# Two MLPs with a Strassen-scheme down-projection on one Trainium2 core: VectorE and ScalarE held to the order of the source, with one sum, gathering or addition behind the split of each plain tile

## The chip, the core and the metric

The kernel runs on one core of one Trainium2 chip. The metric is device time in microseconds (us) of one execution; the time before is the median of three runs, 2092.59 us (2090.18 to 2093.03). Engines are named as the profile names them: PE is TensorE's matmul, PEld its weight load, DVE is VectorE, ACT is ScalarE, POOL is GpSimd, SP is SyncE, which here only issues DMAs.

## What is computed

Two layers of a transformer trunk over 256 tokens of width 2048, in fp32. Layer 0 mixes tokens by stick-breaking attention, layer 1 by an indexer that selects keys for a softmax attention. Behind each mixer stands the MLP, which is what the change touches:

```python
SEQ, D_MODEL = 256, 2048
D_FF = 4 * D_MODEL
for i in range(DEPTH):                       # DEPTH = 2
    ...
    h = rms_norm(x, norm_mlp[i])
    x = x + jnp.square(jax.nn.relu(h @ w_up[i])) @ w_down[i]
```

## The kernel before

**Tiles and the split.** All weights stream through the core as tiles of 256 rows by 512 columns (512 KB), each used once. A tile lands in one of five `wraw` buffers (`load`, line 966; issued on SP's queue in program order). `split` (line 978) turns it into two fp32r halves: ACT copies it to `wh` (line 988, recorded as line 87, the helper `copy`), and DVE writes `wl`, the rest, as `raw - wh` (line 989). `wh` and `wl` have three buffers each, and a tile is split two tiles ahead of its use (`LEAD = 2`). PE takes eight matmuls with `wh` and then four with `wl` for a plain tile (`high_first`, line 246), over both halves of the tokens.

**The loop** (line 1008) runs over a flat list of `Item`s, one for each tile. For item i it emits the split of item i+2, the load of item i+7, the matmuls of item i, the functions in `it.post`, and what was put off by `later` (work that turns an activation: `to_features` transposes on DVE, writes the result to DRAM in four DMAs `td<-jx`, reads it back as `jx<-td` four items on, and runs a DVE and an ACT step behind that).

**Order.** The program is built under a scheduler that models the time of each engine and may set an instruction ahead of others on its queue. `keep` (line 80) holds an instruction in the program's order among the others that were kept; `pin` (line 82) does so only for the first 24 items. So in the MLPs before, the splits (`pin`) are placed by the scheduler, and so are the DVE operations of the Strassen scheme.

**The MLP** (`mlp`, line 327) works through d_ff in four quarters f. `up(f)` makes the quarter's activation `hT`, `down(f)` multiplies it by `w_down`, two column blocks of 512 at a time: `down_pair(f, n)` (line 405). Of the quarter's eight row blocks, blocks 0 and 2 (`SEVEN`) are done for both column blocks and both token halves by Strassen's seven products in place of eight. A pair is 19 tiles: twelve plain ones, `G0` to `G5` and `H0` to `H5` (twelve matmuls each, line 419), and the seven products `s1` to `s7` (six matmuls each, line 437). `s1`, `s2`, `s3` use tiles as they are, `s5`, `s6`, `s7`, `s4` use sums of tiles:

- `t1` (line 464): X = Y - raw(s1), where Y is a fourth tile, loaded by itself (`load_y`);
- `t2` (line 467): Z = raw(s3) - X; `t3` (line 468): Y = raw(s3) - Y; `t4` (line 471): Z = raw(s2) - Z;
- s5 takes X, s6 and later s4 take Z, s7 takes Y. They are split like any tile, but have no load.

The products of s1, s6, s5, s7 are gathered from PSUM into E: `p1` (an ACT copy, line 475), `p6` (line 478), `p5` (line 481), `p7` (line 485). `into(t)` (line 491) adds E to the residual `xs`, and `down_done` (line 361) adds the plain accumulators, by `add_residual` (line 309). `sums(f)` (line 387) builds the sums of activations once a quarter. The order of a pair's tiles is the list `TURNS` (line 49):

```python
TURNS = "G0 H0 s1 G1 s3 H1 G2 s6 s5 H2 s7 G3 H3 s2 G4 H4 s4 G5 H5".split()
```

There are 15 pairs: two in each of four quarters in layer 0, and seven in layer 1, whose last two column blocks are done plainly. In layer 0's last quarter `add_residual` also turns the finished columns for the next mixer (`turn`, line 188). In the first pair of quarters 0 to 2 there is still work of the up-projection left: two times the squared ReLU (line 347), the ACT copy (line 352) and the DVE rest (line 357), and a pair of transposes (line 167).

Of the kernel before, what the change touches and what calls it, by code (L numbers as in the profile page):

```python
# [9 lines left out]
F32 = mybir.dt.float32  # L10
# [7 lines left out]
P = 128  # L18
# [27 lines left out]
WARM = 8  # L46
SEVEN = (0, 2)
STEP = KB * (SEVEN[1] - SEVEN[0])
TURNS = "G0 H0 s1 G1 s3 H1 G2 s6 s5 H2 s7 G3 H3 s2 G4 H4 s4 G5 H5".split()


class Item:
# [2 lines left out]

    def __init__(self, src, a, b, mm):
        self.src, self.a, self.b, self.mm, self.post = src, a, b, mm, []
        self.form, self.after, self.early = None, None, []


@with_exitstack
def trunk(ctx, tc, x, x_t, gains_t, w_in_a, w_out_a, w_in_b, w_out_b, rel_bias, w_up, w_down, out):
# [23 lines left out]
    def copy(o, i, scale=1.0):  # L86
        pin(act.activation(o, i, AF.Copy, scale=scale))  # L87
# [168 lines left out]
    def tokens_out(items, key, w, r0, c0, lhs, q, done, apart=False, alone=False):  # L256
# [25 lines left out]
        def mm(wh, wl):  # L282
# [10 lines left out]
            for t, j, part, wx, a, z in high_first(wh, wl):  # L293
# [2 lines left out]
                    start=a and q == 0, stop=z and q == (end if t else QB) - 1))  # L296
        it = Item(rows(w, r0 + KB * P * q, KB * P, c0, 512), KB, 512,
                  mm if len(items) >= LEAD else first)
        if q == QB - 1:
            it.post.append(lambda: done(accs.pop(key)))  # L300
        items.append(it)
# [25 lines left out]
    def mlp(l, next_col):  # L327
# [77 lines left out]
        def down_pair(f, n):  # L405
# [22 lines left out]
            def seventh(left, src, to=None, done=None):  # L428


                def mm(wh, wl):
                    if to is None:
                        p = auxp.tile([P, 512], F32, name="aux")
                    else:
                        p = accs[keys[to[0]]][to[1]]
                    for t, j, part, wx, a, z in high_first(wh, wl, 1):
                        keep(pe.matmul(p, left(part, j), wx[:, j, :], start=to is None and a,  # L437
                                       stop=to is None and z))
                    if done is not None:
                        done(p)  # L440
# [19 lines left out]
            def load_y():  # L460
                keep(nc.sync.dma_start(new("Y"), block(1, qa)))

            def t1(b11):
                dve.tensor_sub(new("X"), sec["Y"], b11)  # L464

            def t2_t3(b22):
                dve.tensor_sub(new("Z"), b22, sec["X"])
                dve.tensor_sub(sec["Y"], b22, sec["Y"])

            def t4(b21):  # L470
                dve.tensor_sub(sec["Z"], b21, sec["Z"])  # L471

            def p1(p):
                sec["E"] = sec["pool"].tile([P, 4, 512], F32, name="E", bufs=1)
                copy(sec["E"][:, 0], p)

            def p6(p):
                dve.tensor_add(sec["E"][:, 1], p, sec["E"][:, 0])

            def p5(p):  # L480
                dve.tensor_add(sec["E"][:, 2], p, sec["E"][:, 1])

            def p7(p):
                E = sec["E"].rearrange("p (a b) e -> p a b e", a=2)
                dve.tensor_add(E[:, :, 1], p.unsqueeze(1).to_broadcast([P, 2, 512]),
                               sec["E"][:, 1:3])

            def into(t):
                xc = xs[:, t, 1024 * n:1024 * n + 1024].rearrange("p (c e) -> p c e", c=2)
                E = sec["E"].rearrange("p (c t) e -> p c t e", t=2)[:, :, t]  # L490
                dve.scalar_tensor_tensor(xc, E, sec["rs2"][:, t:t + 1], xc, op0=OP.mult, op1=OP.add)

            qa, qb = SEVEN
            seven = {
                "s1": seventh(own(qa, 0), block(0, qa), None, p1),
                "s2": seventh(own(qb, 0), block(0, qb), (0, 0)),
                "s3": seventh(summed(3), block(1, qb), (1, 0)),
                "s4": seventh(own(qb, 1), "Z", (0, 1)),
                "s5": seventh(summed(0), "X", None, p5),
                "s6": seventh(summed(1), "Z", None, p6),  # L500
                "s7": seventh(summed(2), "Y", None, p7)}
# [476 lines left out]
    def split(i, a=slice(None)):  # L978
        if i < len(items):
            it = items[i]  # L980
            raw = raws[i] if it.form is None else it.form()
            if it.form is None and a.stop in (None, it.a):
                raws.pop(i)
            if i not in parts:
                parts[i] = [wpool.tile([P, WT], F32R, name=name)[:, :it.a * it.b].rearrange(
                    "p (a b) -> p a b", a=it.a) for name in ("wh", "wl")]
            wh, wl = parts[i]
            copy(wh[:, a], raw[:, a])
            pin(dve.tensor_sub(wl[:, a], raw[:, a], wh[:, a].bitcast(F32)))  # L989
# [66 lines left out]
```

## Time and profile before

| | |
|---|---|
| median of three runs | 2092.59 us |
| time of the profiled execution | 2085.87 us |
| its span, first to last instruction | 2084.2 us |
| mean granted TensorE clock | 0.999 |
| ACT busy, share of the span | 49% |
| POOL busy, share of the span | 1% |
| DMA, mean | 223 GB/s |

The profile is of one execution. A busy time on PE is a sum over instructions that overlap: a matmul is recorded with some 390 ns, and the next one starts 227 ns behind it. "Idle before" is the time an engine stood still ahead of an instruction, and the name behind the arrow is what ended that. In the timeline, neighbouring instructions of a kind are merged into one row with their count.

### The profile page before, as it was taken

The page shows a single profiled execution, that of the slowest core. Times are in us where ns is not written, and L with a number is a line of the kernel's source. Part 1 is how long each engine was busy: PE and PEld are TensorE (multiplying, and loading weights), DVE is VectorE, ACT ScalarE, POOL GpSimd, SP SyncE. Part 2 cuts the span into 40 slices and gives each one's busy share as a digit, 9 for nine tenths or more (in the row PEclk, how much of TensorE's full clock was granted, in tenths as well). Part 3 has the DMA queues.
Part 4 walks back from the last instruction along what each step waited for, and adds up shares of the span by engine and source line. Part 5 has one row for each costly group of instructions (what it writes and reads, how often), then busy time and mean ns, then how long its engine had stood idle before and what let it go on. Part 6 is the DMA issues. An engine that isn't in the chain of part 4 may idle for free. (4 is left out here: it accounts for less than half of the span.)

```text
span 2084.2 us, 24925 instructions
## 1 busy us (share of the span) xinstructions
PE 2062.2 (99%) x9164; PEld 1696.2 (81%) x9164; DVE 1449.8 (70%) x1581; ACT 1025.5 (49%) x1233; POOL 29.0 (1%) x71
## 2 busy tenths in 40 slices
PE   9999999999999999999999999999999999999999
PEld 7888888888878878878877788888887887888787
DVE  5555655666686687688785798676668667867875
ACT  6555554544454444455454566554445444444543
POOL 0010100000000000000000000000000000000000
PEclk9999999999999999999999999999999999999999
DMA  9878847887856866776588688497876687577554
GB/s 314 241 224 223 240 154 227 242 253 231 248 197 198 261 200 199 235 220 204 192 231 250 198 246 260 151 269 231 253 238 216 198 236 229 191 218 246 194 198 164
DMA packets 477467, 464.85 MB, mean 223 GB/s; under 512 B 269664, under 2 KB 279968, under 8 KB 477344
## 3 DMA queue, kind: packets, MB, share of 16 engines
q1 hardware_dynamic: 469488, 455.81, 71.5%
q10 hardware_dynamic: 7856, 7.45, 1.3%
q8 instruction: 72, 1.18, 0.2%
q14 instruction: 51, 0.42, 0.1%
HBM read 425.90 MB, written 37.22 MB: 222 GB/s over the span
## 5 line engine op out<-in xcount | busy, mean ns | idle before, releaser
L87 ACT ACTIVATE wh<-wraw 128x1024 fp32r<-128x1024 f32 (+1 forms) x725 | 765.6, 1057 | 887.0 <-PE acc L294 571.8
L989 DVE TENSOR_TENSOR wl<-wraw,wh 128x1024 fp32r<-128x1024 f32 (+1 forms) x725 | 877.1, 1218 | 433.9 <-ACT wh L87 417.4
L294 PE MATMUL acc<-wh,xT 128*128 128x512 f32 x3264 | 811.7, 390 | 2.3 <-ACT xT L198 2.3
L294 PEld LDWEIGHTS acc<-wh,xT 128*128 128x128 f32 x3264 | 610.8, 188 | 130.5 <-ACT xT L198 2.5
L294 PE MATMUL acc<-wl,xT 128*128 128x512 f32 x1632 | 437.4, 390 | 0.0
L294 PEld LDWEIGHTS acc<-wl,xT 128*128 128x128 f32 x1632 | 306.2, 188 | 64.1 <-DVE wl L989 0.3
L419 PE MATMUL acc<-wh,hT 128*128 128x512 f32 x1440 | 357.1, 390 | 0.0
L419 PEld LDWEIGHTS acc<-wh,hT 128*128 128x128 f32 x1440 | 271.2, 188 | 57.4
L419 PE MATMUL acc<-wl,hT 128*128 128x512 f32 x720 | 194.0, 391 | 2.0 <-DVE wl L989 1.9
L419 PEld LDWEIGHTS acc<-wl,hT 128*128 128x128 f32 x720 | 134.1, 188 | 34.0 <-DVE wl L989 6.6
L294 PE MATMUL acc<-wh,oT 128*128 128x512 f32 x512 | 128.9, 391 | 0.0
L294 PEld LDWEIGHTS acc<-wh,oT 128*128 128x128 f32 x512 | 95.5, 188 | 19.8
L294 PE MATMUL acc<-wl,oT 128*128 128x512 f32 x256 | 69.5, 392 | 0.0
L167 DVE STREAM_TRANSPOSE jx<-acc 128x512 f32<-128x512 f32 x68 | 44.6, 695 | 34.5 <-PE acc L294 31.9
L294 PEld LDWEIGHTS acc<-wl,oT 128*128 128x128 f32 x256 | 47.8, 188 | 9.8
L471 DVE TENSOR_TENSOR Z<-wraw,Z 128x1024 f32<-128x1024 f32 x15 | 18.4, 1226 | 44.9 <-DMA wraw<-in_w_down_dram 44.9
L437 PE MATMUL aux<-wh,S 128*128 128x512 f32 x180 | 48.2, 389 | 0.0
L87 ACT ACTIVATE wh<-Z 128x1024 fp32r<-128x1024 f32 x30 | 31.9, 1063 | 27.9 <-PE acc L437 17.2
L352 ACT ACTIVATE hT<-jx 128x1024 fp32r<-128x1024 f32 x32 | 33.8, 1055 | 23.4 <-DVE jx L347 23.4
L464 DVE TENSOR_TENSOR X<-Y,wraw 128x1024 f32<-128x1024 f32 x15 | 18.4, 1226 | 36.9 <-DMA wraw<-in_w_down_dram 36.9
L309 DVE SCALAR_TENSOR_TENSOR xs<-acc,rs,xs 128x512 f32<-128x512 f32 x56 | 39.3, 743 | 5.0 <-PE acc L419 5.0
L989 DVE TENSOR_TENSOR wl<-Z,wh 128x1024 fp32r<-128x1024 f32 x30 | 36.7, 1223 | 7.5 <-ACT wh L87 7.4
(191 smaller groups left out, 1275.1 us busy)
## 6 DMA issues: line engine op xcount, KB each, us to landing
wraw<-in_w_up_dram SPq DMA_DIRECT2D x256, 512.0 KB, 4.3
wraw<-in_w_down_dram SPq DMA_DIRECT2D x241, 512.0 KB, 4.8
wraw<-in_w_in_a_dram SPq DMA_DIRECT2D x94, 512.0 KB, 4.5
wraw<-in_w_in_b_dram SPq DMA_DIRECT2D x64, 512.0 KB, 4.4
td<-jx SPq DMA_DIRECT2D x240, 128.0 KB, 4.3
jx<-td SPq DMA_DIRECT2D x45, 512.0 KB, 6.2
wraw<-in_w_out_a_dram SPq DMA_DIRECT2D x32, 512.0 KB, 4.3
wraw<-in_w_out_b_dram SPq DMA_DIRECT2D x32, 512.0 KB, 4.6
```

The source lines that it names most:

```text
L87: pin(act.activation(o, i, AF.Copy, scale=scale))
L167: dve.transpose(y[:, m:m + k, :].rearrange("p k f -> p (k f)"), part)
L294: (keep if alone else pin)(pe.matmul(acc[t], L[:, KB * q + j, part, t * P:(t + 1) * P], wx[:, j, :], start=a and q == 0, stop=z and q == ( ...
L309: dve.scalar_tensor_tensor(xc, acc[t], scale[:, t:t + 1], xc, op0=OP.mult, op1=OP.add)
L352: keep(act.activation(h, r, AF.Copy))
L419: keep(pe.matmul(acc[t], L[:, KB * qs[i] + j, part, t * P:(t + 1) * P], wx[:, j, :], start=a and i == 0, stop=z and i == len(qs) - 1))
L437: keep(pe.matmul(p, left(part, j), wx[:, j, :], start=to is None and a, stop=to is None and z))
L464: dve.tensor_sub(new("X"), sec["Y"], b11)
L471: dve.tensor_sub(sec["Z"], b21, sec["Z"])
L989: pin(dve.tensor_sub(wl[:, a], raw[:, a], wh[:, a].bitcast(F32)))
```

## The change

Four things are changed. `TURNS` sets `H2` between s6 and s5, and s5 and s7 each behind another plain tile. The splits of all MLP tiles are kept in program order on ACT and DVE (`it.alone`, set for the tiles of `up`, of the plain column blocks and of the pairs), and so are `t1` to `t4`, `p1`, `p6`, `p5`, `p7` and `into`. These no longer hang on the split or the product that they belong to (`it.after`, `done`), but on named tiles of the pair, one behind each, through `it.post.insert(0, step)`. And `t2` and `t3`, which were one function, are two.

```diff
-TURNS = "G0 H0 s1 G1 s3 H1 G2 s6 s5 H2 s7 G3 H3 s2 G4 H4 s4 G5 H5".split()
+TURNS = "G0 H0 s1 G1 s3 H1 G2 s6 H2 s5 G3 s7 H3 s2 G4 H4 s4 G5 H5".split()
...
-            def t1(b11):
-                dve.tensor_sub(new("X"), sec["Y"], b11)
-
-            def t2_t3(b22):
-                dve.tensor_sub(new("Z"), b22, sec["X"])
-                dve.tensor_sub(sec["Y"], b22, sec["Y"])
...
+            def t1():
+                keep(dve.tensor_sub(new("X"), sec["Y"], seven["s1"].raw))
+
+            def t2():
+                keep(dve.tensor_sub(new("Z"), seven["s3"].raw, sec["X"]))
+
+            def t3():
+                keep(dve.tensor_sub(sec["Y"], seven["s3"].raw, sec["Y"]))
...
-            seven["s1"].after, seven["s3"].after, seven["s2"].after = t1, t2_t3, t4
             for name in TURNS:
                 it = seven[name] if name in seven else plain("GH".index(name[0]), int(name[1]))
+                it.alone = True
                 items.append(it)
             items[base - 8].early.append(load_y)
-            for t in range(2):
-                items[base + TURNS.index(("G3", "H3")[t])].post.append(lambda t=t: into(t))
+            for name, step in (("H0", t1), ("s1", p1), ("G1", t2), ("H1", t3), ("H2", p6), ("G3", p5),
+                               ("H3", t4), ("G4", p7), ("H4", lambda: into(0)),
+                               ("G5", lambda: into(1))):
+                items[base + TURNS.index(name)].post.insert(0, step)
...
-            copy(wh[:, a], raw[:, a])
-            pin(dve.tensor_sub(wl[:, a], raw[:, a], wh[:, a].bitcast(F32)))
-            if it.after is not None:
-                it.after(raw)
+            order = keep if it.alone else pin
+            order(act.activation(wh[:, a], raw[:, a], AF.Copy))
+            order(dve.tensor_sub(wl[:, a], raw[:, a], wh[:, a].bitcast(F32)))
+            it.raw = raw
```

The two programs have the same number of instructions of each kind on each engine. How DVE's queue is ordered by them is shown at three places. In the rows below a tile's buffer carries a running number; a split is the row that writes `wl`, and its `wraw` says which tile it is. Line numbers of the changed kernel are larger by up to seven.

The first place is DVE's queue at the start of the first pair of layer 0's second quarter. Before: `wraw_5509` is G0, 5528 H0, 5547 s1, 5565 G1, 5585 s3.

```order
L464 TENSOR_TENSOR X_5643<-Y_5485,wraw_5547 128x1024
L989 TENSOR_TENSOR wl_5600<-wraw_5509,wh_5599 128x1024
L347 SCALAR_TENSOR_TENSOR jx_5579<-jx_5579 128x1024
L467 TENSOR_TENSOR Z_5685<-wraw_5585,X_5643 128x1024
L468 TENSOR_TENSOR Y_5485<-wraw_5585,Y_5485 128x1024
L989 TENSOR_TENSOR wl_5618<-wraw_5528,wh_5617 128x1024
L167 STREAM_TRANSPOSE jx_5635<-acc_5487 128x512 x2
L989 TENSOR_TENSOR wl_5640<-wraw_5547,wh_5639 128x1024
L989 TENSOR_TENSOR wl_5664<-wraw_5565,wh_5663 128x1024
L357 TENSOR_TENSOR hT_5339<-jx_5579,hT_5339 128x2x4x128
L989 TENSOR_TENSOR wl_5682<-wraw_5585,wh_5681 128x1024
```

Now, at the same place, 5547 again being s1, 5565 G1, 5585 s3, 5603 H1, 5621 G2, and the split of `Z` the one for s6:

```order
L996 TENSOR_TENSOR wl_5640<-wraw_5547,wh_5639 128x1024
L348 SCALAR_TENSOR_TENSOR jx_5579<-jx_5579 128x1024
L996 TENSOR_TENSOR wl_5662<-wraw_5565,wh_5661 128x1024
L464 TENSOR_TENSOR X_5680<-Y_5485,wraw_5547 128x1024
L996 TENSOR_TENSOR wl_5684<-wraw_5585,wh_5683 128x1024
L358 TENSOR_TENSOR hT_5339<-jx_5579,hT_5339 128x2x4x128
L996 TENSOR_TENSOR wl_5698<-wraw_5603,wh_5697 128x1024
L467 TENSOR_TENSOR Z_5715<-wraw_5585,X_5680 128x1024
L996 TENSOR_TENSOR wl_5718<-wraw_5621,wh_5717 128x1024
L996 TENSOR_TENSOR wl_5730<-Z_5715,wh_5729 128x1024
L470 TENSOR_TENSOR Y_5485<-wraw_5585,Y_5485 128x1024
```

`t1`, which reads s1's tile, stood ahead of the splits of G0, H0 and s1 itself, and now stands behind those of s1 and G1; `t2` and `t3`, which read s3's tile, stood ahead of the split of H0, and now stand behind those of H1 and s6.

The second place is DVE's queue in the middle of the same pair. Before, `wraw_5752` is s2, 5688 H2, 5720 G3, `jx` is an activation on its way to the squared ReLU:

```order
L989 TENSOR_TENSOR wl_5717<-wraw_5621,wh_5716 128x1024
L989 TENSOR_TENSOR wl_5731<-Z_5685,wh_5730 128x1024
L989 TENSOR_TENSOR wl_5749<-X_5643,wh_5748 128x1024
L471 TENSOR_TENSOR Z_5685<-wraw_5752,Z_5685 128x1024
L989 TENSOR_TENSOR wl_5767<-wraw_5688,wh_5766 128x1024
L478 TENSOR_TENSOR E_5697<-aux_5772,E_5697 128x512
L989 TENSOR_TENSOR wl_5781<-Y_5485,wh_5780 128x1024
L481 TENSOR_TENSOR E_5697<-aux_5786,E_5697 128x512
L347 SCALAR_TENSOR_TENSOR jx_5728<-jx_5728 128x1024
L989 TENSOR_TENSOR wl_5796<-wraw_5720,wh_5795 128x1024
```

Now, with 5701 G3, 5733 H3, 5752 s2, 5770 G4, 5783 H4:

```order
L996 TENSOR_TENSOR wl_5780<-wraw_5701,wh_5779 128x1024
L480 TENSOR_TENSOR E_5694<-aux_5772,E_5694 128x512
L348 SCALAR_TENSOR_TENSOR jx_5727<-jx_5727 128x1024
L996 TENSOR_TENSOR wl_5800<-Y_5485,wh_5799 128x1024
L996 TENSOR_TENSOR wl_5812<-wraw_5733,wh_5811 128x1024
L483 TENSOR_TENSOR E_5694<-aux_5803,E_5694 128x512
L358 TENSOR_TENSOR hT_5339<-jx_5727,hT_5339 128x2x4x128
L996 TENSOR_TENSOR wl_5832<-wraw_5752,wh_5831 128x1024
L996 TENSOR_TENSOR wl_5847<-wraw_5770,wh_5846 128x1024
L473 TENSOR_TENSOR Z_5715<-wraw_5752,Z_5715 128x1024
L996 TENSOR_TENSOR wl_5866<-wraw_5783,wh_5865 128x1024
L996 TENSOR_TENSOR wl_5878<-Z_5715,wh_5877 128x1024
```

`t4`, which reads s2's tile, stood ahead of the splits of H2, s7, G3, H3 and s2 itself, and now stands behind those of s2 and G4. Between `p6` and `p5`, where one split stood, there are two.

The third place is DVE's queue where layer 0's MLP ends and the second mixer begins (`acc_7915` and `acc_7936` are the last two column blocks, `xs` the residual, the transposes of `xs` feed the turn for the mixer; `wraw_8152` and `wraw_8164` are the mixer's second and third tile). Before:

```order
L309 SCALAR_TENSOR_TENSOR xs_89<-acc_7915,rs2_3294,xs_89 128x512 x2
L989 TENSOR_TENSOR wl_8237<-wraw_8152,wh_8236 128x1024
L167 STREAM_TRANSPOSE jx_8228<-xs_89 128x512 x2
L309 SCALAR_TENSOR_TENSOR xs_89<-acc_7936,rs2_3294,xs_89 128x512 x2
L691 TENSOR_TENSOR gqk_8281<-gains_74 128x1
L989 TENSOR_TENSOR wl_8284<-wraw_8164,wh_8283 128x1024
L167 STREAM_TRANSPOSE jx_8256<-xs_89 128x512 x2
```

Now, the first column block being `acc_7913`:

```order
L310 SCALAR_TENSOR_TENSOR xs_89<-acc_7913,rs2_3294,xs_89 128x512
L996 TENSOR_TENSOR wl_8237<-wraw_8149,wh_8236 128x1024
L310 SCALAR_TENSOR_TENSOR xs_89<-acc_7913,rs2_3294,xs_89 128x512
L167 STREAM_TRANSPOSE jx_8228<-xs_89 128x512
L310 SCALAR_TENSOR_TENSOR xs_89<-acc_7936,rs2_3294,xs_89 128x512 x2
L697 TENSOR_TENSOR gqk_8281<-gains_74 128x1
L996 TENSOR_TENSOR wl_8284<-wraw_8161,wh_8283 128x1024
L167 STREAM_TRANSPOSE jx_8228<-xs_89 128x512
L167 STREAM_TRANSPOSE jx_8256<-xs_89 128x512 x2
```

The addition of the first block and its transposes, which stood together but for one split, are taken apart: half of the addition, a split, the other half, one transpose, the second block's addition, another split, the other transpose. On SP's queue the load that stood between the two writes of the turned columns now stands ahead of both, and in layer 0's last pair the write of the second block turned there has moved ahead of two loads. In the other pairs SP's order is as it was.

More of the change, by code (lines that the diff above doesn't have):

```diff
@@ L57, in __init__ @@
         self.src, self.a, self.b, self.mm, self.post = src, a, b, mm, []
-        self.form, self.after, self.early = None, None, []
+        self.form, self.early, self.alone, self.raw = None, [], False, None
 @with_exitstack
@@ L298, in tokens_out @@
                   mm if len(items) >= LEAD else first)
+        it.alone = alone
         if q == QB - 1:
@@ L426, in plain, with seventh @@
                 return it
-            def seventh(left, src, to=None, done=None):
+            def seventh(left, src, to=None):
                 def mm(wh, wl):
@@ L438, in mm @@
                                        stop=to is None and z))
-                    if done is not None:
-                        done(p)
+                    it.product = p
                 own_rows = not isinstance(src, str)
@@ L461, in load_y, with t4, p1, p6 @@
                 keep(nc.sync.dma_start(new("Y"), block(1, qa)))
-            def t1(b11):
-                dve.tensor_sub(new("X"), sec["Y"], b11)
-            def t2_t3(b22):
-                dve.tensor_sub(new("Z"), b22, sec["X"])
-                dve.tensor_sub(sec["Y"], b22, sec["Y"])
-            def t4(b21):
-                dve.tensor_sub(sec["Z"], b21, sec["Z"])
-            def p1(p):
-                sec["E"] = sec["pool"].tile([P, 4, 512], F32, name="E", bufs=1)
[L475 to L483, printed above, removed]
+            def t1():
[4 more added lines that the diff above has]
+                keep(dve.tensor_sub(sec["Y"], seven["s3"].raw, sec["Y"]))
+            def t4():
+                keep(dve.tensor_sub(sec["Z"], seven["s2"].raw, sec["Z"]))
+            def p1():
+                sec["E"] = sec["pool"].tile([P, 4, 512], F32, name="E", bufs=1)
+                keep(act.activation(sec["E"][:, 0], seven["s1"].product, AF.Copy))
+            def p6():
+                keep(dve.tensor_add(sec["E"][:, 1], seven["s6"].product, sec["E"][:, 0]))
+            def p5():
+                keep(dve.tensor_add(sec["E"][:, 2], seven["s5"].product, sec["E"][:, 1]))
+            def p7():
                 E = sec["E"].rearrange("p (a b) e -> p a b e", a=2)
-                dve.tensor_add(E[:, :, 1], p.unsqueeze(1).to_broadcast([P, 2, 512]),
-                               sec["E"][:, 1:3])
+                keep(dve.tensor_add(E[:, :, 1],
+                                    seven["s7"].product.unsqueeze(1).to_broadcast([P, 2, 512]),
+                                    sec["E"][:, 1:3]))
             def into(t):
@@ L490, in into @@
                 E = sec["E"].rearrange("p (c t) e -> p c t e", t=2)[:, :, t]
-                dve.scalar_tensor_tensor(xc, E, sec["rs2"][:, t:t + 1], xc, op0=OP.mult, op1=OP.add)
+                keep(dve.scalar_tensor_tensor(xc, E, sec["rs2"][:, t:t + 1], xc,
+                                              op0=OP.mult, op1=OP.add))
             qa, qb = SEVEN
             seven = {
-                "s1": seventh(own(qa, 0), block(0, qa), None, p1),
+                "s1": seventh(own(qa, 0), block(0, qa)),
                 "s2": seventh(own(qb, 0), block(0, qb), (0, 0)),
```

6 lines of the change are left out of this document (3 added, 3 removed).

## The prediction, made before the changed kernel had run

> **What bounds the kernel now.** The page's part 1 comes first, then the list of waits of DVE, then PE over the stretches in which the down-projections run.
>
> ```profile
> PE 2062.2 (99%) x9164; PEld 1696.2 (81%) x9164; DVE 1449.8 (70%) x1581; ACT 1025.5 (49%) x1233; POOL 29.0 (1%) x71
> ...
> core 0: us, PE busy (x), PEclk, DMA share, GB/s
> 556.95:643.00 86.05, 84.94 (x374) 1.00 0.63 202
> ...
> sum 656.44, PE 641.53; mean PE 106.92
> ...
> 702.84 1.98 PE L294 MATMUL acc<-wh,xT 128*128 128x512 f32 x8
> ...
> 721.88 1.98 PE L294 MATMUL acc<-wh,xT 128*128 128x512 f32 x8
> ...
> 735.48 1.07 PE L437 MATMUL aux<-wh,hT 128*128 128x512 f32 x4
> 736.38 0.61 PE L437 MATMUL aux<-wl,hT 128*128 128x512 f32 x2
> 736.84 1.98 PE L419 MATMUL acc<-wh,hT 128*128 128x512 f32 x8
> ```
>
> PE is the bound. In the up-projection seven plain tiles lie between 702.84 and 721.88: 2.720 us each, 0.2267 us for a matmul; a product of Strassen's scheme, with six, takes 1.36 (735.48 to 736.84). The six stretches in which L419 and L437 run alone (15 pairs of 12 x 12 + 7 x 6 = 186 matmuls, 2790 in all) have 656.44 us. At 0.2267 they would need 632.4. So **24.0 us are lost in the pairs**, and nothing that keeps PE's work can gain more there.
>
> ```profile
> DVE Z L471 <- DMA wraw<-in_w_down_dram: 44.9, 15, 3.8
> DVE X L464 <- DMA wraw<-in_w_down_dram: 36.9, 15, 4.1
> ...
> DVE Z L467 <- DMA wraw<-in_w_down_dram: 4.6, 5, 1.6
> ...
> 749.08 1.23 DVE L471 TENSOR_TENSOR Z<-wraw,Z 128x1024 f32<-128x1024 f32 x1 [3.83 <-DMA wraw<-in_w_down_dram]
> 750.23 1.22 DVE L989 TENSOR_TENSOR wl<-wraw,wh 128x1024 fp32r<-128x1024 f32 x1
> 751.36 0.68 DVE L478 TENSOR_TENSOR E<-aux,E 128x512 f32<-128x512 f32 x1
> ...
> 751.50 1.20 PE L419 MATMUL acc<-wl,hT 128*128 128x512 f32 x4 [0.45 <-DVE wl L989]
> ```
>
> Who loses them is read here. DVE stood 86.4 us before `t4`, `t1` and `t2`, once or more in each of the 15 pairs, waiting for tiles that PE needs much later. At 749.08 it had waited 3.83 us for s2's tile, with H2's split queued behind; that split ended at 751.45, and PE's four `wl` matmuls of H2 began at 751.50.
>
> **What the change takes away.** `t1` to `t4` now stand behind the split of the tile that they read, so that tile has landed when they come up, and the 86.4 us of waits go. What is late next is DVE's own work, so I walk through one pair. A `wl` may start when ACT's `wh` is done, and that starts when PE has left the buffer:
>
> ```profile
> 702.13 1.06 ACT L87 ACTIVATE wh<-wraw 128x1024 fp32r<-128x1024 f32 x1 [1.66 <-PE acc L294]
> ...
> 703.22 1.23 DVE L989 TENSOR_TENSOR wl<-wraw,wh 128x1024 fp32r<-128x1024 f32 x1 [1.49 <-ACT wh L87]
> ...
> 736.58 1.07 ACT L87 ACTIVATE wh<-wraw 128x1024 fp32r<-128x1024 f32 x1 [0.75 <-PE aux L437]
> ```
>
> Against the start of PE's tile i, ACT starts the split of tile i+2 0.71 us ahead behind a plain tile (702.13 to 702.84) and 0.26 ahead behind a product (736.58 to 736.84). PE needs a plain tile's `wl` 1.81 us into it (eight matmuls), a product's 0.91 us into it. DVE's operations are these; back to back they follow each other some 0.09 us closer than their durations (750.23 to 751.36 for one of 1.22):
>
> ```profile
> L989 DVE TENSOR_TENSOR wl<-wraw,wh 128x1024 fp32r<-128x1024 f32 (+1 forms) x725 | 877.1, 1218 | 433.9 <-ACT wh L87 417.4
> L167 DVE STREAM_TRANSPOSE jx<-acc 128x512 f32<-128x512 f32 x68 | 44.6, 695 | 34.5 <-PE acc L294 31.9
> L471 DVE TENSOR_TENSOR Z<-wraw,Z 128x1024 f32<-128x1024 f32 x15 | 18.4, 1226 | 44.9 <-DMA wraw<-in_w_down_dram 44.9
> L309 DVE SCALAR_TENSOR_TENSOR xs<-acc,rs,xs 128x512 f32<-128x512 f32 x56 | 39.3, 743 | 5.0 <-PE acc L419 5.0
> ...
> L357 DVE TENSOR_TENSOR hT<-jx,hT 128x1024 fp32r<-128x1024 f32 x32 | 39.0, 1218 | 0.0
> L347 DVE SCALAR_TENSOR_TENSOR jx<-jx 128x1024 f32<-128x1024 f32 x32 | 38.9, 1215 | 1.9 <-DMA jx<-td 1.9
> L491 DVE SCALAR_TENSOR_TENSOR xs<-E,rs,xs 128x1024 f32<-128x1024 f32 x30 | 38.4, 1279 | 0.0
> ...
> L478 DVE TENSOR_TENSOR E<-aux,E 128x512 f32<-128x512 f32 x15 | 10.3, 684 | 0.0
> L485 DVE TENSOR_TENSOR E<-aux,E 128x1024 f32<-128x1024 f32 x15 | 18.3, 1218 | 0.0
> ```
>
> The fullest kind of pair is the first of a quarter: 19 splits, 4 `t`, `p7` and 4 leftover operations of 1.22 us, 2 `into` of 1.28, 4 additions of 0.74, `p6` and `p5` of 0.68, 2 transposes of 0.70: 42.4 us by durations, 39.1 at the closer pace of its 37 rows, against 42.2 us of PE (186 x 0.2267). With the new rows of DVE, PE's tiles at G0 0, H0 2.72, s1 5.44, G1 6.80, s3 9.52, H1 10.87 and so on, and DVE busy with transposes until 1.44, the walk gives the end of `wl` against PE's need:
>
> | tile | s1 | H1 | s6 | s7 | H3 | s2 | H4 | s4 | G5 |
> |---|---|---|---|---|---|---|---|---|---|
> | `wl` done | 2.6 | 9.9 | 13.4 | 22.6 | 24.9 | 27.8 | 31.2 | 32.4 | 34.6 |
> | needed | 6.4 | 12.7 | 17.2 | 25.4 | 27.6 | 29.4 | 34.4 | 36.2 | 38.5 |
>
> The closest is s2, with 1.6 us left; DVE ends the pair 1.4 us behind its plain rhythm and has caught up two tiles on. Second pairs lack the leftover 4.9 us and are looser. `sums(3)`, partly in a first pair, puts 0.1 us more on the way there, since DVE waits for ACT later anyway. The one pair that fails by the same walk is layer 0's last, with eight more 0.48 us operations of the turn and four transposes: its s7, H3 and s2 come out 0 to 0.3 us late, and ACT has to wait for a turned block ahead of s7. I leave 0.5 us for that (bounds 0 and 3), and 1.0 of the 24.0 us as unevenness that no wait explains.
>
> `p6`, `p5` and ACT's `p1` wait for a product of PE with splits queued behind: `p6` comes up at 19.6 and its product is done at 17.9; `p1` holds ACT 0.4 us and takes 0.6, and the next `wh` is not needed for 3 us. Nothing (bounds 0 and 1). On SP, H3's load now waits for `t3`, and that of the next pair's G0 for `t4`, with loads behind them:
>
> ```profile
> wraw<-in_w_down_dram SPq DMA_DIRECT2D x241, 512.0 KB, 4.8
> ...
> 741.19 17.58 SPq L972 DMA_DIRECT2D wraw<-in_w_down_dram  x6
> ```
>
> `t3` ends at 14.4 and ACT is ready for H3 at 22.6: 8.1 us for a load whose median is 4.8, and which at worst, in the bunch issued from 741.19 on, had landed by 749.08, after at most 7.9. Nothing (bound: rival 2).
>
> **The entry of the second mixer** is the one place that gets worse.
>
> ```profile
> 1081.64 1.41 DVE L309 SCALAR_TENSOR_TENSOR xs<-acc,rs,xs 128x512 f32<-128x512 f32 x2 [0.85 <-PE acc L419]
> ...
> 1084.10 1.30 DVE L167 STREAM_TRANSPOSE jx<-xs 128x512 f32<-128x512 f32 x2
> ...
> 1085.42 7.63 SPq L173 DMA_DIRECT2D td<-jx  x4
> 1093.17 0.59 SPq L972 DMA_DIRECT2D wraw<-in_w_in_b_dram  x1
> 1093.86 5.54 SPq L173 DMA_DIRECT2D td<-jx  x4
> ...
> 1108.56 2.33 PE L294 MATMUL acc<-wh,xT 128*128 128x512 f32 x9 [2.25 <-ACT xT L198]
> ```
>
> Here the first transposes end 3.8 us behind the first product (1081.64 to 1085.4). Now they come behind half an addition (0.7), a split (1.1), the other half, a transpose (1.3), the second block's addition, which waits for its own product 2.7 us on (1.4 from then), a split and a transpose: about 6.2 us. The load between the writes (0.7) goes ahead, so the chain of writes, read and `xT`, for which PE waited 2.25 us, ends about 1.6 us later. I take 1.6 (bounds 0, if the writes are shorter, and 4).
>
> **A rule on the clock.** The longest wait in the pairs was followed by slow matmuls:
>
> ```profile
> 1035.72:1084.16 48.44, 44.22 (x187) 35.84 (x186) 39.66 (x45) 27.09 (x40) 0.00 (x0) 0.96 0.73 219
> ...
> 1063.07 1.22 PE L437 MATMUL aux<-wl,S 128*128 128x512 f32 x2 [2.39 <-DVE wl L989]
> 1064.09 3.01 PE L419 MATMUL acc<-wh,hT 128*128 128x512 f32 x8
> ```
>
> From 1063.07 to 1064.09 two matmuls take 1.02 us in place of 0.45, the eight behind them are slow for a while too, and the granted clock of the stretch is 0.96. These some 1.6 us are in the 24.0 and, hung on the wait, go with it. The Trainium skill, "TensorE: Matmul & The Clock Gate", section "What's actually happening", has the gate close only after an idle window of about 3.4 us. By that a wait of 2.39 us isn't the cause and the 1.6 us would stay, an estimate of 19.3 us of gain in place of 20.9; the row shows the slow clock right behind the wait, and I go by the row.
>
> **The sum.** -24.0 + 1.0 + 0.5 + 1.6 = -20.9 us. The profiled execution took 2085.87 us, its span 2084.2 and 1.7 around it: 2065.0. The median of the three runs is 6.7 us above that execution; the gain is the same number of matmuls' waits in both, so from 2092.59 it gives **2071.7 us**.
>
> **Rivals.**
> 1. *DVE becomes the bound.* For: 39.1 of 42.2 us, and each wait for ACT adds to it. Against: the walk has those waits. By durations, 42.4 us exceed PE's 42.2; with the walk's waits of some 2.7 us the seven fullest pairs (first pairs of quarters 0 to 2 in both layers, layer 0's last) would each lose 3 us less the 1.6 of slack, plus what it costs to catch up, say 1.7: 12 us come back, 2084. In the Trainium skill, "VectorE: DVE Perf Modes", section "The DRAIN you can't avoid", the next operation doesn't start until the pipe is empty; by that the durations would count. Rows 750.23 and 751.36 show it starting 0.09 us before the recorded end. Chance 0.13.
> 2. *Loads come late, and it is slower.* `t3` and `t4` hold the buffers of s3 and s2 longer, and SP's queue is in order. To end over 4.2 us slower, the 15 pairs must lose 24.0 + 4.2, 1.9 us each. PE needs H3's `wh` at 25.8, so its load must start by 16.8 even at 7.9 us; `t3` would have to end after 18.7, 4.3 us behind the walk. Price at that point: 2097 and above. Chance 0.06.
> 3. *The order is not what cost the time.* If DVE, without the DMA waits, only waits for ACT instead and the same splits are late, nothing moves: 2092.6. Against: PE's stall at 751.50 follows the DMA wait directly. Chance 0.06.
>
> The forecast has 0.75. What a measurement of this kernel can tell from no change is about 0.2%, 4.2 us. Faster by more: 0.75 + 0.13 = 0.88; within: 0.06; slower: 0.06. The range takes in the bounds of the unknown costs (-24.0 and 2 us of spread below; rival 1 above): 2067 to 2084, leaving out rivals 2 and 3.
>
> **What would show it.** Right: no DVE wait for a DMA before `t1` to `t4`; PE's pairs at some 634 us in the six stretches in place of 656; PE's wait for `xT` at the mixer's entry 3 to 4 us. Wrong: PE waiting for `wl` at s2 or H3 in first pairs (rival 1), or ACT waiting for `wraw` of `w_down` (rival 2).

## The result, and the profile after

The changed kernel takes 2063.95 us (median of four, 2063.33 to 2066.02); the kernel before, beside it, 2091.39 us (four, 2090.17 to 2093.03). The ratio is 0.987, 95% interval 0.9853 to 0.9887: 24 to 31 us faster. That is 7.8 us below the predicted 2071.7 and 3 us below the low end of the range.

Part 1 of the page, then the list of PE's waits (engine, tile and line, what was waited for: us in total, times, longest):

```profile
PE 2053.8 (100%) x9164; PEld 1697.1 (82%) x9164; DVE 1453.9 (71%) x1581; ACT 1025.4 (50%) x1233; POOL 28.9 (1%) x71
```

```profile
PE acc L294 <- ACT xT L198: 2.1, 1, 2.1
PE acc L123 <- DVE ones L95: 1.1, 1, 1.1
PE acc L267 <- ACT wh L995: 0.8, 2, 0.5
PE acc L420 <- DVE wl L996: 0.2, 1, 0.2
```

Before, PE stood 14.9 us for `wl` of the pairs (7.6 + 5.4 + 1.9, lines 437 and 419); 0.2 us is left, and no wait of DVE for a tile of `w_down` is in the list any more. PE over the stretches in which the pairs run (us, PE busy, granted clock, DMA share, GB/s):

```profile
core 0: us, PE busy (x), PEclk, DMA share, GB/s
557.65:641.97 84.32, 84.32 (x373) 1.00 0.66 205
...
900.37:1068.95 168.58, 168.38 (x742) 1.00 0.69 212
...
sum 633.25, PE 633.04; mean PE 90.44
```

The first quarter's two pairs take 84.32 us, which is 372 matmuls of 0.2267 us and nothing else. All six stretches take 633.25 us in place of 656.44, against the 632.4 that 2790 matmuls need: **0.85 us is lost where 24.0 were**, and all of it in layer 0's last pair. The span outside the pairs is 1428.3 us, and was 1427.7.

DVE's timeline at the place shown for before (start, duration, instruction):

```profile
749.27 1.22 DVE L348 SCALAR_TENSOR_TENSOR jx<-jx 128x1024 f32<-128x1024 f32 x1
750.41 1.22 DVE L996 TENSOR_TENSOR wl<-Y,wh 128x1024 fp32r<-128x1024 f32 x1
752.56 1.23 DVE L996 TENSOR_TENSOR wl<-wraw,wh 128x1024 fp32r<-128x1024 f32 x1 [0.94 <-ACT wh L995]
753.71 0.68 DVE L483 TENSOR_TENSOR E<-aux,E 128x512 f32<-128x512 f32 x1
754.31 1.22 DVE L358 TENSOR_TENSOR hT<-jx,hT 128x1024 fp32r<-128x1024 f32 x1
755.44 2.35 DVE L996 TENSOR_TENSOR wl<-wraw,wh 128x1024 fp32r<-128x1024 f32 x2
757.71 1.22 DVE L473 TENSOR_TENSOR Z<-wraw,Z 128x1024 f32<-128x1024 f32 x1
```

`t4` (line 473) starts with no wait. The pair began at 729.01, so s7's `wl` is done 22.6 us in (751.63) and s2's 27.6 us in (756.66; the first of the two splits at 755.44): the walk had 22.6 and 27.8.

### The profile page after: what moved, and what is told of

The parts are those of the page before. It is cut to its first block, busy times and chain, and to the rows that moved or that the text cites. A ratio compares the mean times of both kernels' runs of the same rounds, so it can differ in the third digit from the quotient of the medians.

```text
span 2061.5 us, 24939 instructions
## 1 busy us (share of the span) xinstructions
PE 2053.8 (100%) x9164; PEld 1697.1 (82%) x9164; DVE 1453.9 (71%) x1581; ACT 1025.4 (50%) x1233; POOL 28.9 (1%) x71
## 3 DMA queue, kind: packets, MB, share of 16 engines
q8 instruction: 72, 1.18, 0.2%
## 5 line engine op out<-in xcount | busy, mean ns | idle before, releaser
L438 PEld LDWEIGHTS aux<-wh,S 128*128 128x128 f32 x180 | 33.8, 188 | 7.0
L358 DVE TENSOR_TENSOR hT<-jx,hT 128x1024 fp32r<-128x1024 f32 x32 | 39.0, 1218 | 0.0
```

Of the source, the lines that this page charges most:

```text
L358: keep(dve.tensor_sub(l, r, h.bitcast(F32)))
```

## The experiments

In what follows the *loss* of a run is the time of the pairs in its profiled execution less 632.4 us, worked out from the starts of its matmuls. It is split into the six **first** pairs (of quarters 0 to 2, both layers), the **last** pair of layer 0, and the eight **others**.

| run | time, us (runs) | ratio to before | loss | first | others | last |
|---|---|---|---|---|---|---|
| before, profiled | 2085.87 (1) | | 24.0 | 12.5 | 5.2 | 6.3 |
| after | 2063.95 (4) | 0.987 [0.9853, 0.9887] | 0.85 | 0 | 0 | 0.85 |
| before_again | 2086.51 (11) | 0.9999 [0.999, 1.0008] | 25.0 | 15.2 | 2.4 | 7.4 |
| splits_kept | 2089.64 (10) | 1.002 [1.0011, 1.0029] | 27.5 | 18.9 | 0.5 | 8.1 |
| turns_only | 2082.56 (10) | 0.9983 [0.9974, 0.9992] | 17.9 | 9.0 | 3.4 | 5.6 |
| t_only | 2065.18 (4) | 0.990 [0.9886, 0.9913] | 1.6 | 0.9 | 0 | 0.7 |
| t123_only | 2070.87 (4) | 0.9921 [0.9905, 0.9938] | 9.3 | 7.5 | 0 | 1.8 |
| t4_only | 2074.06 (4) | 0.994 [0.9925, 0.9954] | 11.9 | 0.5 | 1.0 | 10.4 |
| t4_early | 2067.12 (4) | 0.9907 [0.9888, 0.9927] | 3.0 | 0 | 0 | 3.0 |
| t123_early | 2094.0 (9) | 1.0033 [1.002, 1.0045] | 29.2 | 6.8 | 14.2 | 8.3 |
| p6x4 | 2076.34 (1) | | 14.0 | 7.9 | 0 | 6.1 |
| p6x8 | 2117.1 (1) | | 53.6 | 26.6 | 18.3 | 8.7 |
| fill8 | 2121.09 (1) | | 58.4 | 32.5 | 16.8 | 9.2 |
| t3_late | 2065.85 (1) | | 1.7 | 0 | 0 | 1.7 |

The kernel before, run beside them in three groups, took 2085.76 (27 runs, 2080.5 to 2090.68), 2086.76 (12) and 2086.81 us (7).

### Which part of the change does it

Four runs take the change apart. `before_again` is the kernel before. `t_only` has the splits and `t1` to `t4` kept in the new manner, but the old `TURNS` and the gathering as before. `splits_kept` changes only the order of the splits, `turns_only` only the list:

```diff
 splits_kept
-            copy(wh[:, a], raw[:, a])
-            pin(dve.tensor_sub(wl[:, a], raw[:, a], wh[:, a].bitcast(F32)))
+            order = keep if it.alone else pin
+            order(act.activation(wh[:, a], raw[:, a], AF.Copy))
+            order(dve.tensor_sub(wl[:, a], raw[:, a], wh[:, a].bitcast(F32)))
 turns_only
-TURNS = "G0 H0 s1 G1 s3 H1 G2 s6 s5 H2 s7 G3 H3 s2 G4 H4 s4 G5 H5".split()
+TURNS = "G0 H0 s1 G1 s3 H1 G2 s6 H2 s5 G3 s7 H3 s2 G4 H4 s4 G5 H5".split()
 t_only, against the changed kernel
-            for name, step in (("H0", t1), ("s1", p1), ("G1", t2), ("H1", t3), ("H2", p6), ("G3", p5),
-                               ("H3", t4), ("G4", p7), ("H4", lambda: into(0)),
-                               ("G5", lambda: into(1))):
+            for name, step in (("H0", t1), ("s1", p1), ("G1", t2), ("H1", t3), ("s6", p6), ("s5", p5),
+                               ("H3", lambda: into(1)), ("H3", t4), ("s7", p7), ("G3", lambda: into(0))):
```

> The kernel before, unchanged, to see what its ordinary executions lose. Theory A (the time is lost by DVE waiting for tiles ahead of t1 to t4, and how long depends on when the tiles land): the excess of PE in the six stretches of pairs over 2790 matmuls x 0.2267 differs from execution to execution, 24 us where the execution takes 2086 and 28 to 30 where it takes 2090 to 2092, and the span outside the pairs stays at 1628 within 1 us. Theory B (the ordinary executions carry some 5 us outside the pairs, at the start, the end or in the mixers): the pairs lose 24 us whatever the execution takes, and the rest of the span is 1632 or so where the execution takes 2090.

> The old order of tiles; splits and t1 to t4 kept in the source's order, t1 to t4 behind the split of their tile; p1, p6, p5, p7 and the additions of E left to the scheduler as before. Theory A: all DMA waits of DVE ahead of t1 to t4 go and with them nearly all that the change gained: pairs lose 0 to 3 us, time 2064 to 2067. Theory C (the spreading of the gathering operations and the new order of tiles are needed as well): pairs lose 8 us or more, time over 2071.

> The kernel before with only the splits of the MLPs kept in the source's order; t1 to t4 stay where the scheduler puts them, ahead of the splits of their tiles. Theory A: the DMA waits stay at 80 to 90 us, pairs lose 22 to 30 us, time 2085 to 2093, no change. Theory D (it is the scheduler's order of the splits themselves that cost the time): time 2064 to 2070.

> The kernel before with only the new order of tiles (TURNS). Theory A: t1 to t4 stay ahead of the splits of their tiles, DMA waits 80 to 90 us, but s6 and s5 are no longer neighbours, so the splits behind the wait for s2's tile are needed a little later: pairs lose 15 to 28 us, time 2080 to 2092. Theory C: at least half of the gain, time 2064 to 2077.

(In the first of these, 1628 is a slip of arithmetic for some 1428, 2084.2 less 656.4.) The profiled execution of `before_again` took 2087.08 us, 1.2 more than the one before it; its pairs lose 25.0 us and the rest takes 1427.9, which is theory A's way. But it is none of the executions of 2090 us and more that theory A and B differ about. The lists of DVE's waits of `splits_kept` and then `turns_only`, and the sum over the pairs of `t_only`:

```profile
DVE Z L472 <- DMA wraw<-in_w_down_dram: 39.0, 14, 4.4
DVE X L465 <- DMA wraw<-in_w_down_dram: 27.4, 15, 3.7
```

```profile
DVE Z L471 <- DMA wraw<-in_w_down_dram: 44.0, 15, 3.7
DVE X L464 <- DMA wraw<-in_w_down_dram: 32.6, 15, 3.5
```

```profile
sum 634.00, PE 633.37; mean PE 90.48
```

In the first two, DVE goes on waiting ahead of the sums, and both keep most of the loss. In `t_only` there is no such wait and 1.6 us of loss. So the place of the four sums behind the splits is what the gain comes from, on top of splits in the source's order; the sums moved without kept splits were not run. Keeping the splits alone makes it 0.1 to 0.3% slower; the new `TURNS` alone gains 0.1 to 0.3%.

### Which of the sums

`t4_early` and `t123_early` take the changed kernel and put one part back; `t123_only` and `t4_only` take `t_only` and hang the other part on its split again.

```diff
 t4_early
-                               ("H3", t4), ("G4", p7), ("H4", lambda: into(0)),
+                               ("s6", t4), ("G4", p7), ("H4", lambda: into(0)),
 t123_early
-            for name, step in (("H0", t1), ("s1", p1), ("G1", t2), ("H1", t3), ("H2", p6), ("G3", p5),
+            for name, step in (("s1", p1), ("H2", p6), ("G3", p5),
...
+            for at, step in ((-3, t1), (-2, t3), (-2, t2)):
+                items[base + at].post.insert(0, step)
 t123_only, against t_only
-                keep(dve.tensor_sub(sec["Z"], seven["s2"].raw, sec["Z"]))
+                dve.tensor_sub(sec["Z"], b21, sec["Z"])
...
+            seven["s2"].after = t4
 t4_only, against t_only
+            seven["s1"].after, seven["s3"].after = t1, t2_t3
```

> The changed kernel with one step put back: t4 stands right behind the split of s5's neighbour s6 (as before, ahead of the splits of H2, s5, G3, s7, H3 and s2) and not behind that of G4; all else as changed. Its tile s2 is read from the moment it has landed. Theory A (a sum that reads a tile not yet landed holds DVE's queue, and the wl behind it come late): DVE again waits some 40 to 50 us in all ahead of t4, up to 4 us in each of 15 pairs, and the pairs, which lose 1 us in the changed kernel, lose 8 to 18: span outside the pairs 1428, time 2071 to 2082. Rival B (with the tiles spread out by the new TURNS and everything in order, DVE has enough spare time to wait): the wait appears, PE does not, time 2064 to 2066.

> The changed kernel with the other three sums put back: t1 is emitted three tiles ahead of the pair, t2 and t3 two tiles ahead, as they stood in the kernel before; t4 stays behind G4's split. Theory A: DVE waits some 30 to 45 us in all for s1's and s3's tiles at the start of the pairs, and since G0's and H0's wl stand behind them, the pairs lose 4 to 12 us: time 2067 to 2076. Rival B (at a pair's start PE's need of wl is 4 to 6 us away, as the walk has it for s1, so a wait of 4 us is made up): the waits are there and the time is 2064 to 2066; then it was t4 alone that cost the time before.

> The kernel before with the splits kept and t1, t2, t3 kept behind the splits of H0's, G1's and H1's later tiles, as in the run with all four sums moved; t4 hangs on its split again, without an order of its own, so that the scheduler sets it. Theory A1 (each sum costs what DVE waits for it: t4's 45 us of waits are half of the 86): about half of the gain is there, pairs' loss 8 to 14, time 2072 to 2078. Theory A2 (the early sums delay the splits that free the buffers, and t4's waits are mostly a consequence of that): t4's waits fall below 15 us, pairs' loss 1 to 5, time 2065 to 2069, nearly the whole gain.

> The counterpart: splits kept, t4 kept behind H3's tile's turn, t1, t2 and t3 hung on their splits and set by the scheduler as before. Theory A1: DVE waits about 40 us ahead of t1 and t2, none at t4; pairs' loss 8 to 14, time 2072 to 2078. Theory A2: the waits at the pair's start stay, the loads stay late, and most of the loss with them: pairs' loss 16 to 25, time 2080 to 2090. If neither run alone gains anything near half, the waits add up only together.

`t4_early` came out as its rival had it, and the place that the expectation names is two splits off: `t4` stands behind those of H2 and s5, and came up 17.9 us into a pair. DVE waited for s2's tile once, 2.9 us, not 15 times:

```profile
DVE Z L473 <- DMA wraw<-in_w_down_dram: 2.9, 1, 2.9
```

That is no return to the old place: before, `t4` came up 15.2 us into the first pair of layer 0's second quarter and waited until 19.05 (3.83 us, as shown in the prediction). And s2's tile had landed by then, because the loads ahead of it came earlier and less bunched (us from the pair's start, issue to landing; after is the changed kernel, and `t4_early` has s2's tile at 16.8):

| load of | H2 | G3 | H3 | s2 |
|---|---|---|---|---|
| before | 8.2 to 13.5 | 8.9 to 14.7 | 11.2 to 17.7 | 11.6 to 19.0 |
| after | 4.9 to 9.6 | 6.1 to 11.2 | 9.8 to 14.4 | 12.1 to 16.7 |

SP's queue shows why, before and then after (the pair begins at 730.03 and 729.01). The four writes of the last activations stand ahead of these loads and wait for DVE's transposes, which stood behind `t1` to `t3`:

```profile
734.04 4.10 SPq L173 DMA_DIRECT2D td<-jx  x4
738.25 1.13 SPq L972 DMA_DIRECT2D wraw<-in_w_down_dram  x2
```

```profile
730.55 3.15 SPq L173 DMA_DIRECT2D td<-jx  x4
733.93 1.84 SPq L978 DMA_DIRECT2D wraw<-in_w_down_dram  x2
```

s2's own load went out no later before (11.6 against 12.1) and landed 2.3 us later, behind the bunch. So in this pair it seems that the early sums made `t4`'s tile late as well, over two queues; this is read from the one pair's rows, and no run held the loads alone.

`t123_early` is slower than the kernel before, by another way than expected. DVE waits only 33.6 us there (14.8 for X, 18.8 for Z), yet the eight other pairs, which lost 5.2 before, lose 14.2. DVE's and then PE's timeline of it:

```profile
772.59 1.22 DVE L467 TENSOR_TENSOR Z<-wraw,X 128x1024 f32<-128x1024 f32 x1 [1.06 <-DMA wraw<-in_w_down_dram]
773.73 1.22 DVE L470 TENSOR_TENSOR Y<-wraw,Y 128x1024 f32<-128x1024 f32 x1
774.87 1.28 DVE L494 SCALAR_TENSOR_TENSOR xs<-E,rs,xs 128x1024 f32<-128x1024 f32 x1
776.06 1.41 DVE L310 SCALAR_TENSOR_TENSOR xs<-acc,rs,xs 128x512 f32<-128x512 f32 x2
```

```profile
777.61 1.63 PE L420 MATMUL acc<-wh,hT 128*128 128x512 f32 x6 [1.43 <-DVE xs L310]
```

Behind the waiting sums stand the additions of the pair before (line 310), and these free the accumulators that PE needs for H0, 2.7 us into the pair. PE's list has 12.0 us in eight waits for line 310. So the sums and their wait cost some 1.8 us in each of the eight pairs, and through what was queued behind them.

The halves are about what A1 expected in loss (9.3 and 11.9; A1 8 to 14), though `t4`'s waits in `t123_only` fell to 12.6 us, below the 15 that A2 named; and the losses sit in different pairs. With `t1` to `t3` early (`t4_only`), DVE waits 28.0 us for X, and the 14 pairs besides layer 0's last lose 1.5 us together. With `t4` left to the scheduler (`t123_only`), these 12.6 us of waits come with 7.5 us of loss in the first pairs, most of it in one wait at H3 in each. The walk and the trace of the changed kernel fit that: at a pair's start a `wl` is done 3.7 to 5.6 us ahead of its need, around s2 1.8. Of the 10.4 us of `t4_only` in layer 0's last pair some 3.4 are waits for `wl` at H0 and s1. The other 7 come over ACT, whose timeline has this:

```profile
1055.32 1.71 ACT L198 ACTIVATE xT<-jx,gains 128x256 fp32r<-128x256 f32 x4 [3.73 <-DMA jx<-td]
1056.93 2.94 ACT L991 ACTIVATE wh<-wraw 128x1024 fp32r<-128x1024 f32 x3
```

Its step of the turn waited for the block read back, with G3's `wh` queued behind, and PE waited 3.96 us for that; 12 slow matmuls followed. Where only some operations are kept, the scheduler sets the others anew, so the halves are no clean shares of the gain.

### How much room DVE has

`p6x4` and `p6x8` repeat `p6`; `fill8` repeats another addition of the same size, which reads no PSUM.

```diff
 p6x4 (p6x8: range(9))
-                keep(dve.tensor_add(sec["E"][:, 1], seven["s6"].product, sec["E"][:, 0]))
+                for _ in range(5):
+                    keep(dve.tensor_add(sec["E"][:, 1], seven["s6"].product, sec["E"][:, 0]))
 fill8
+                for _ in range(8):
+                    keep(dve.tensor_add(sec["E"][:, 2], sec["E"][:, 0], sec["E"][:, 1]))
```

> The changed kernel with p6 done five times in place of once (the same sum, 128x512, some 0.6 us each back to back): 2.4 us more of DVE in each of 15 pairs, ahead of the splits of s7, H3 and s2. It measures the slack that the walk gave as 1.6 us at s2 in the fullest pairs. By the walk: PE waits 0.8 us for wl in each of the six first pairs of quarters 0 to 2 in both layers, some 2.4 us more in layer 0's last pair, nothing in the others: pairs' loss 1.2 + 5 + 2 = about 8 us, time 2069 to 2073. Rival (the walk is too tight, DVE has 3 us or more at s2): pairs' loss below 3, time under 2066. Rival (DVE is the bound already): every pair loses about 2.4, time 2095 and above.

> As before, with p6 done nine times: 4.8 us more of DVE in each pair. By the walk: some 3 us lost in each of the six fullest pairs, 5 in layer 0's last, and 0 to 1 in each of the eight others: 23 to 31 us, time 2085 to 2096. Rival (more slack than the walk has): under 2075. Between this and the run with 2.4 us, the slope says whether DVE's time passes one to one into the pairs once the slack is gone.

> The changed kernel with eight more additions on DVE behind p6, of the same size as p6 but from E alone into a part of E that p5 overwrites: 4.8 to 5 us more of DVE in each pair at the place where the run with p6 nine times had them, but s6's product is read once and its PSUM buffer comes free as in the changed kernel. That run lost 54 us, and in its waits PE stood 27.6 us for p6. If those were the buffer's doing: pairs' loss 23 to 31, as the walk has it, time 2085 to 2096. If the buffer is no matter and DVE's time alone does it: 50 to 55, time 2112 to 2118.

The lists of PE's waits of `p6x8` and then of `fill8`, and DVE's timeline of `fill8`:

```profile
PE aux L438 <- DVE E L481: 27.6, 15, 4.2
PE aux L438 <- DVE wl L997: 7.5, 7, 1.5
```

```profile
PE aux L438 <- DVE wl L998: 38.2, 15, 6.0
```

```profile
576.96 0.68 DVE L480 TENSOR_TENSOR E<-aux,E 128x512 f32<-128x512 f32 x1
577.67 5.78 DVE L482 TENSOR_TENSOR E<-E 128x512 f32<-128x512 f32 x8
583.37 1.22 DVE L348 SCALAR_TENSOR_TENSOR jx<-jx 128x1024 f32<-128x1024 f32 x1
```

The PSUM buffer, which `p6x8` seems to wait for 15 times, is no matter: without it the same 15 waits go to `wl` and the loss is as large. It was only the first of two things that were late together: in a first pair of `p6x8` the buffer holds PE 1.82 us at s7's first matmul and `wl` another 1.18 at its fifth, in `fill8` `wl` alone holds it 3.10 at the fifth. The expectation missed the size (23 to 31 us) because the filler is longer than I reckoned: eight additions that each wait for the one ahead take 5.78 us, 0.72 each, not 0.6. Against that the walk holds. It gave s7 2.8 us of room in a first pair, and 5.78 - 2.8 is 3.0; PE waited 3.1 to 3.2 us there, in each of the six. In the others the changed kernel's trace has 3.4 us of room; that leaves 2.4, and they wait 1.96. With four (2.9 us), PE waits 0.2 us for s7, and the first pairs lose 1.3 us each, which is 2.9 less the walk's 1.6 at s2. `p6x4` all the same took 2076.34 us and lost 14.0, where 2069 to 2073 and about 8 were expected: the filler's length puts 3 us more into the first pairs, and layer 0's last pair lost 6.1 in place of some 3, with a dozen slow matmuls in it. Once the room is used up, DVE's time passes into PE's almost one to one, and behind the waits of 3.1 to 3.2 us slow matmuls and later waits add 1.7 to 3.0 us a pair.

### A tile held longer

```diff
 t3_late
-("G1", t2), ("H1", t3), ("H2", p6)
+("G1", t2), ("H2", t3), ("H2", p6)
```

> The changed kernel with t3 set one plain tile later, behind the split that follows H2's turn, so that s3's buffer, and with it H3's load, comes free some 6 us later (t3 ends at about 20.5 in the walk in place of 14.4). It tests the price of the rival in which loads come late. By the walk PE needs H3's wh at 25.8 and the load takes 4.7: ACT waits for wraw of w_down in most of the 15 pairs and the pairs lose 9 to 55 us, time 2073 to 2120. Rival (the load has more room than the walk gives): no ACT wait for w_down beyond 5 us, time 2063 to 2066.

No loss in the pairs beside layer 0's last, and ACT's list of waits has one wait for a tile of `w_down`, of 3.4 us. DVE's timeline and SP's, around H1's split and around `t3`:

```profile
737.16 1.23 DVE L996 TENSOR_TENSOR wl<-wraw,wh 128x1024 fp32r<-128x1024 f32 x1 [0.28 <-ACT wh L995]
...
748.85 1.21 DVE L470 TENSOR_TENSOR Y<-wraw,Y 128x1024 f32<-128x1024 f32 x1
```

```profile
738.42 0.37 SPq L978 DMA_DIRECT2D wraw<-in_w_down_dram  x1
...
750.09 0.37 SPq L978 DMA_DIRECT2D wraw<-in_w_down_dram  x1
```

H3's load, which the walk hung on `t3`, is the one at 738.42: it goes when H1's split is done (738.39). The one behind `t3` is G5's, needed 15 us later. So the five buffers are not handed on in turn in this program; H3's load took the one that came free.

### Where the kernel before scatters

Its times lie between 2080.5 and 2093.0 us, the four of the changed kernel within 3 us. Three more profiled executions of the unchanged kernel were to say whether that scatter lies in the pairs.

> The kernel before, once more, with a profile. Its times scatter over 10 us (2080.5 to 2093 so far), those of the changed kernel over 3. Theory A (the scatter is in the pairs: each DMA that lands later or earlier lengthens a wait of DVE or not): the span outside the pairs is again 1427 to 1429, and all of this look's difference to the others is in the pairs, whatever its time. Theory B (a slower or faster stretch of the whole execution, an offset that the changed kernel has too): the pairs have 656 to 658 as in the two profiles so far, and the rest moves with the time.

> The same kernel and the same theories as the look before it: A, outside the pairs 1427 to 1429 and the difference in the pairs; B, pairs 656 to 658 and the difference outside.

> The same kernel and the same theories as the two looks before it: A, outside the pairs 1427 to 1429 and the difference in the pairs; B, pairs 656 to 658 and the difference outside.

They took 2086.65, 2088.42 and 2082.79 us. The sums over the pairs of the second and the third:

```profile
sum 656.53, PE 641.13; mean PE 106.85
```

```profile
sum 652.58, PE 640.76; mean PE 106.79
```

Over all five profiled executions of this kernel the pairs take 652.6 to 657.4 us, the rest 1427.7 to 1430.2. The fastest is fast in its pairs (rest 1428.4), the slowest is slow outside them (1430.2, against the first execution 1.2 us more at the second mixer and 1.2 ahead of the first pair). So neither theory has it alone: both parts move, the pairs twice as much. No execution above 2089 us left a profile.

## Why the prediction missed

**The mechanism: right.** The waits ahead of `t1` to `t4` cost the time, they are gone, and nothing took their place. `t_only`, `splits_kept` and `turns_only` show that it is the sums' place and not the rest of the change.

**The size in the pairs: right to 0.7 us.** -24.0 + 1.0 + 0.5 was the forecast, -22.5; -23.2 was measured. The 1.0 us of unevenness does not exist: 14 of the 15 pairs run without any loss. Layer 0's last pair loses 0.85 in place of 0.5. (The fullest pair has 38 rows by the prediction's own list, not 37, which moves its 39.1 us by 0.1.) The walk, tile by tile, against the trace of the changed kernel (layer 0's first pair, us from its start):

| `wl` done | s1 | H1 | s6 | s7 | H3 | s2 | H4 | s4 | G5 |
|---|---|---|---|---|---|---|---|---|---|
| walk | 2.6 | 9.9 | 13.4 | 22.6 | 24.9 | 27.8 | 31.2 | 32.4 | 34.6 |
| trace | 2.6 | 9.9 | 13.4 | 22.6 | 24.8 | 27.6 | 31.1 | 32.4 | 34.6 |

And in layer 0's last pair, where it had s7, H3 and s2 0 to 0.3 us late, PE is held 0.2 us at s7 and 0.3 at H3.

**The entry of the second mixer: +1.6 us forecast, none measured.** SP's timeline of the changed kernel, ACT's, and PE's wait:

```profile
1074.70 10.27 SPq L173 DMA_DIRECT2D td<-jx  x8
...
1087.03 0.46 SPq L179 DMA_DIRECT2D jx<-td  x1
```

```profile
1093.52 1.71 ACT L198 ACTIVATE xT<-jx,gains 128x256 fp32r<-128x256 f32 x4
```

```profile
1094.08 2.34 PE L294 MATMUL acc<-wh,xT 128*128 128x512 f32 x9 [2.08 <-ACT xT L198]
```

And the same read and `xT` before:

```profile
1101.45 0.46 SPq L179 DMA_DIRECT2D jx<-td  x1
```

```profile
1107.99 1.71 ACT L198 ACTIVATE xT<-jx,gains 128x256 fp32r<-128x256 f32 x4
```

The path was the one walked: writes, read, `xT`. The read takes 6.5 us from issue to landing both times, and `xT` starts within 0.1 us of that. The transposes of the first block end even later than walked, 6.2 us behind the start of its addition (1068.40) but 7.4 behind its product, since DVE was busy when the product was done; before it was 3.8. But the eight writes then go in one run of 10.3 us, where two runs with a load between them took 14.0 (1085.42 to 1099.40). So the writes start 3.6 us later and their run is 3.7 us shorter; the step had 2.4 of the one and, but for the load's 0.7, nothing of the other. PE waits 2.08 us in place of 2.25, and not the 3 to 4 us that were forecast. Why the writes go faster in one run was not tried.

**The base: wrong, and this is the step that put the result outside the range.** It is the last step of the sum, from 2065.0 to 2071.7. From the profiled execution, 2085.87 us, the sum gave 2065.0; the changed kernel's profiled execution took 2063.33, its median 2063.95. I then added 6.7 us because the median of three runs was higher, with the reason that "the gain is the same number of matmuls' waits in both". That holds for an offset which both kernels have. It isn't one: in the same set the kernel before took 2090.17 to 2093.03 us and the changed one 2063.33 to 2066.02, which is where `t_only` was too, beside a kernel before of 2085.76. The changed kernel's median stands 0.6 us above its profiled execution, not 6.7, and the gain in that set is 27.4 us. The range's low end had the same fault: it took the 24.0 us lost in one execution for the most that any could lose. What the 6.7 us of the first runs were isn't settled, since they left no profile. The five profiled executions show the pairs' loss moving by 4.8 us from one execution to another and the rest by 2.5, so a part of it in longer waits is likely, and not shown. Against the 46 later runs of the kernel before (2086 us), which were not taken beside the changed kernel, the gain is 22 us, and the sum had 20.9.

**The rivals.** *DVE becomes the bound*: no; 1.8 us are left at the closest tile. `p6x4` shows how near it was: with 2.9 us more of DVE in each pair the pairs lose 14 us again. *Loads come late*: the price was wrong, since H3's load hangs on H1's split and not on `t3`; `t3` can end 21.5 us into the pair without loss. *The order is not what cost the time*: no.

**The rule on the clock**: the row was right. With the 2.39 us wait the slow matmuls behind it went: the 0.85 us that the changed kernel still loses in that pair are two short waits, and the granted clock of the stretches is 1.00. The profiled executions differ by 22.5 us, which is nearer to the 20.9 by the row than to the 19.3 by the rule of the Trainium skill ("TensorE: Matmul & The Clock Gate", section "What's actually happening"), that would have left the slow matmuls in.

## What to carry to other kernels

An operation with slack of its own can still be costly where it stands: on an in-order queue its wait is paid by what is queued behind it, so put it behind the work that is needed first, and look for who waits for that, the next load's buffer included. A walk through one period with durations from the trace, starts back to back and each engine's release points, was right to 0.2 us here; two places it could not see were which buffer a load takes and what a queue does once its entries stand together. And where a kernel's waits hang on landing DMAs, as here, their length may change from one execution to the next (the pairs' loss by 4.8 us). A gain that removes such waits is then better set on the profiled execution, with the range opened by the scatter, than on a difference between runs that is carried over as a constant.

## What the hardware showed beside it

**Slow matmuls behind a wait, but not behind every one.** PE's timeline of `t123_early` at two places:

```profile
1041.87 2.11 PE L420 MATMUL acc<-wh,hT 128*128 128x512 f32 x8 [2.96 <-ACT wh L998]
...
1067.05 1.78 PE L438 MATMUL aux<-wh,S 128*128 128x512 f32 x4 [2.07 <-ACT wh L998]
1068.63 1.05 PE L438 MATMUL aux<-wl,S 128*128 128x512 f32 x2
1069.48 2.64 PE L420 MATMUL acc<-wh,hT 128*128 128x512 f32 x8
```

After 2.96 us the eight matmuls keep nearly their pace (2.11 us against 1.98 undisturbed); after 2.07 us two take 1.05 in place of 0.62, and the eight behind them 2.64. The slow ones start 0.427 us apart in place of 0.227, and there are 4 to 13 of them. Taken from the starts, 17 hold-ups of 2.06 to 6.13 us in the pairs were followed by them, and four were not: 2.49, 2.57, 2.84 and 3.12 us, in four runs (the last is the first row above). Shorter ones go either way too: of the eight hold-ups of 1.82 us in the other pairs of `p6x8` one was followed by seven slow matmuls, of the eight of 1.96 us in `fill8` none, and at the second mixer's entry one of 1.85 us was (`before_look2`) and one of 2.30 was not (`before`). Length alone does not decide it; what else does was not tried. The Trainium skill, "TensorE: Matmul & The Clock Gate", section "What's actually happening", has a free-running window of about 3.4 us, which fits that one length falls either way. That a hold-up of 1.82 us is enough does not fit a window that must be idle throughout.

**Operations on DVE that wait for the one ahead don't overlap it.** Independent neighbours start 0.08 to 0.09 us before the recorded end of the one ahead (749.27 and 750.41 above, for 1.22); the eight additions of `fill8`, which write the same part of `E` and each wait for a semaphore that DVE raises itself, start 0.03 us behind it (5.78 us for eight of 0.69). A price for added work taken from the closer pace was a sixth too low.
